# Gate tiles of four feed-forwards computed in pairs by one level of Strassen's algorithm

## The chip, the cores and the metric

The kernel runs on one core of a Trainium2 chip. The metric is the device time of one execution in microseconds (us). Three executions of the kernel before took 2094.15, 2095.79 and 2096.93 us; the median is 2095.79 us.

## What is computed

The reference is a decoder trunk of two layers over 512 tokens of 1024 channels, all in float32. Each layer is a feed-forward, a mixer (a convolution module in layer 0, sparse attention in layer 1), a second feed-forward and a gated input embedding:

```python
def rms_norm(x, g):
    y = xf * lax.rsqrt(jnp.mean(xf * xf, axis=-1, keepdims=True) + RMS_EPS)
    return y * g
def swiglu(x, wg, wu, wd):
    return (jax.nn.silu(x @ wg) * (x @ wu)) @ wd
for i in range(2):
    x = x + 0.5 * swiglu(rms_norm(x, ffn1_norm[i]), ffn1_w_gate[i], ffn1_w_up[i], ffn1_w_down[i])
    x = x + (conformer_conv if i == 0 else nsa_mixer)(rms_norm(x, mix_norm[i]), ...)
    x = x + 0.5 * swiglu(rms_norm(x, ffn2_norm[i]), ffn2_w_gate[i], ffn2_w_up[i], ffn2_w_down[i])
    gate = jax.nn.sigmoid(rms_norm(x, ple_norm[i]) @ ple_w_gate[i])
    x = x + gate * (p[i] @ ple_w_in[i])
return rms_norm(x, final_norm)
```

So there are four feed-forwards. Their weights are 1024 x 2816 (gate, up) and 2816 x 1024 (down). The change concerns `x @ wg` in all four.

## The kernel before

Activations lie transposed: eight tiles `xs[k]` of 128 channels by 512 tokens. A matrix product keeps a 128 x 128 block of weights stationary on TensorE (PE) and moves a tile of 512 tokens past it. To keep float32's precision with the faster fp32r format, each operand is split in a high part (a rounded copy) and a low part (the difference), and `mm3` issues three matmuls (L254, L255, L256): high by high, high by low, low by high.

Weights come in units of 128 x 1024 (eight blocks), numbered in the order of use. SyncE loads a unit into one of two `raw` buffers. `_split` makes the high part on ScalarE (ACT, L230) and the low part (L231) on GpSimd (POOL) for the feed-forwards, apart from the first six units, which VectorE (DVE) does. High and low parts have five buffers each (`wh`, `wl`), so a unit is split while TensorE works four units earlier.

A feed-forward has 22 gate tiles and 22 up tiles of 24 matmuls each (eight channel blocks by three). They run in two parts, f = 0 to 11 and 12 to 21; after each part come eight down tiles m, each summed over the part's f. VectorE finishes each tile f: gate times R, up times R, their product, and the hidden tile's low part, with Silu and the high part on ScalarE.

R is the RMS norm's factor per token. It isn't applied to x before the products but to their results, so the products need not wait for it. It is made by `rfin` in two steps. Step one: the squares' sum `acc`, in two parts, goes through two matmuls with a matrix of 1/1024 (L355); VectorE takes the diagonals of the result in four pieces (L347), adds epsilon (L357); POOL takes the power (L331). Step two (`spread`): four transposes on TensorE (L363) and a copy on ScalarE (L370). The constant `FIN_AT` puts step one behind the gate tile of f = 1 and step two behind the gate tile of f = 2:

```python
            at = 2 * f - (p is pg)
            if at in FIN_AT:        # FIN_AT = (1, 3)
                next(fin)
```

The order within each engine is made when the program is built, by a scheduler that starts from the order of the code; on the chip each engine then runs its instructions in that order.

The functions that the change touches, and what calls them:

Of the kernel before, what the change touches and what calls it, by code (L numbers as in the profile page):

```python
# [27 lines left out]
CALM_FROM = 6  # L28
CALM = ("ffn", "ple_w_gate", "conv_w_pw2")
# [9 lines left out]
PARTS = (range(0, 12), range(12, 22))  # L39
HU = 1024  # L40
# [15 lines left out]
def plan():  # L56
# [13 lines left out]
    def ffn(n, i):  # L70
        for fs in PARTS:
            for f in fs:
                for nm in ("gate", "up"):
                    for k in range(KD):
                        put((f"ffn{n}_w_{nm}", i, k, f), k, ((f * 128, f * 128 + 128),))
# [66 lines left out]

SMALL = {}
# [18 lines left out]
class Kern:  # L162
    def __init__(self, ctx, tc, aps):
# [12 lines left out]
        self.RAWB, self.HLB = 2, 5  # L176
# [19 lines left out]

    def _load(self, j):
        if KINDS[j] == "r":
            return ()
        return self._pieces_in(j)  # L200

    def _pieces_in(self, j):
        t = self.wpool.tile([128, HU], F32, name=f"raw{j}", tag="raw", bufs=self.RAWB)
# [6 lines left out]
    def pieces(self, j, w):  # L210
        return (slice(0, w // 2), slice(w // 2, w)) if j == 0 else (slice(0, w),)

    def _split(self, j):
        w = sum(x[2] for x in UNITS[j])
        if KINDS[j] == "r":
            t = self.wpool.tile([128, HU], F32, name=f"wr{j}", tag="wh", bufs=self.HLB)
            self.nc.sync.dma_start(t[:, :w], self.a["w"][j, :, :w])
            self.hl[j] = (t, t)
            return
        t = self.raw.pop(j)  # L220
        h = self.wpool.tile([128, HU], F32R, name=f"wh{j}", tag="wh", bufs=self.HLB)
        l = self.wpool.tile([128, HU], F32R, name=f"wl{j}", tag="wl", bufs=self.HLB)
        what = UNITS[j][0][0][0]
        nsa, calm = what.startswith("nsa"), j >= CALM_FROM and what.startswith(CALM)
        eng = self.nc.gpsimd if calm or nsa and j % 4 in L_POOL else self.nc.vector
        for c in self.pieces(j, w):
            if nsa and j % 4 in H_POOL:
                self.nc.gpsimd.tensor_copy(h[:, c], t[:, c])
            else:
                self.nc.scalar.activation(h[:, c], t[:, c], AF.Copy)  # L230
# [3 lines left out]
    def ahead(self, j):  # L234
        while self.next_split < min(j + 1, len(UNITS)):
            while self.next_raw < min(self.next_split + self.RAWB, len(UNITS)):
                drain(self._load(self.next_raw))
                self.next_raw += 1
            self._split(self.next_split)
            self.next_split += 1  # L240
        while self.next_raw < min(self.next_split + self.RAWB, len(UNITS)):
            drain(self._load(self.next_raw))
            self.next_raw += 1

    def block(self, key):
        j, o, w = PLACE[key]
        self.ahead(j + self.HLB - 1)
# [15 lines left out]
    def load_consts(self):  # L263
# [16 lines left out]
        first = [self._load(0), self._load(1)]  # L280
# [20 lines left out]
    def parts(self, k):  # L301
# [5 lines left out]
        h, l = (self.ptile("px", 16, dt=F32R) if self.gname == "ple_norm" else self.slot(F32R) for _ in range(2))  # L307
# [89 lines left out]

    def ffn(self, n, i, nxt):
        nc = self.nc
        X = self.X  # L400
        g, u, d = (f"ffn{n}_w_{s}" for s in ("gate", "up", "down"))
        fin = self.rfin(self.acc)
        for pi, fs in enumerate(PARTS):
            hid = {}

            def finish(f, pg, pu):
                R = self.R
                gr, ur = self.tmp(), self.tmp()
                nc.vector.tensor_tensor(gr, pg, R, op=OP.mult)  # L409
                nc.scalar.activation(gr, gr, AF.Silu)  # L410
                nc.vector.tensor_tensor(ur, pu, R, op=OP.mult)  # L411
                nc.vector.tensor_tensor(ur, ur, gr, op=OP.mult)  # L412
                h, l = self.ptile("hid", 24, dt=F32R), self.ptile("hid", 24, dt=F32R)
                nc.scalar.activation(h, ur, AF.Copy)  # L414
                nc.vector.tensor_tensor(l, ur, h.bitcast(F32), op=OP.subtract)  # L415
                hid[f] = (h, l)

            for f in fs:
                pg, pu = self.bank(), self.bank()
                if f == 0:  # L420
                    for ks in (range(KD - 1), (KD - 1,)):
                        for p, nm in ((pg, g), (pu, u)):
                            for k in ks:
                                self.mm3(p, self.block((nm, i, k, f)), X[k], k == 0, k == KD - 1)
                    wait = [(f, pg, pu)]
                    if 0 in FIN_AT:
                        next(fin)
                    continue
                for p, nm in ((pg, g), (pu, u)):
                    for k in range(KD):  # L430
                        self.mm3(p, self.block((nm, i, k, f)), X[k], k == 0, k == KD - 1)
                    at = 2 * f - (p is pg)
                    if at in FIN_AT:
                        next(fin)
                        if at == FIN_AT[1]:
                            for t in wait:
# [885 lines left out]
```

## Time and profile before

| | |
|---|---|
| median of three runs | 2095.79 us |
| profiled execution | 2095.87 us |
| its span, first to last instruction | 2094.1 us |
| TensorE busy | 2060.0 us, 98% |
| VectorE, ScalarE, GpSimd busy | 956.3, 830.6, 1031.2 us |

The profile names an instruction by engine, line and the program's tiles (out<-in). A matmul's duration in it runs to a modelled end and overlaps the next one's, so what a matmul costs in a stream is read from start to start. PE is TensorE's matmuls, PEld its weight loads. PEclk is the clock that the chip granted to TensorE, as a share of 2.4 GHz.

### The profile page before, as it was taken

Reading aid. Unit: us, or ns where it says so; the run is one execution under the profiler, and the core shown is the slowest. Engines: PE = TensorE matmul, PEld = TensorE weight load, DVE = VectorE, ACT = ScalarE, POOL = GpSimd, SP = SyncE. Lnnn points to the kernel's source line nnn. Section 1 sums busy time; section 2 is a strip of 40 time slices with the busy share of each in tenths; the row PEclk is TensorE's granted clock in tenths of the full one; section 3 lists DMA queues with packets and bytes.
Section 4 is the critical chain, followed back from the end, with each engine's and each line's share of the span. In section 5 each row is a group of like instructions: output and inputs, shape, how many; then the busy total and the mean of one; then the engine's idle time right before and its main releaser. Section 6 shows DMA issues by size and latency. Waiting matters only on the chain. (4 is left out here: it accounts for less than half of the span.)

```text
span 2094.1 us, 25510 instructions
## 1 busy us (share of the span) xinstructions
PE 2060.0 (98%) x9608; PEld 1709.4 (82%) x9608; DVE 956.3 (46%) x1744; ACT 830.6 (40%) x1394; POOL 1031.2 (49%) x646
## 2 busy tenths in 40 slices
PE   8999999999999999999999999999999999999998
PEld 7888888888788888887888888887888788888887
DVE  5430334597634303336432133346989653213334
ACT  5321334663533222334332223326888643223333
POOL 2444443686345444444444445647666444444442
PEclk9999999999999999999999999999999999999999
DMA  4332333244273222233332333453323033233232
GB/s 164 100 101 92 100 98 99 94 133 151 101 208 121 92 100 96 96 101 105 101 101 92 99 97 99 161 164 111 91 82 106 32 116 101 95 97 101 92 100 76
DMA packets 77322, 223.29 MB, mean 107 GB/s; under 512 B 8624, under 2 KB 16592, under 8 KB 77200
## 3 DMA queue, kind: packets, MB, share of 16 engines
q1 hardware_dynamic: 76208, 219.26, 32.8%
q0 software_dynamic: 848, 2.34, 0.3%
q8 instruction: 76, 1.25, 0.3%
q14 instruction: 46, 0.38, 0.1%
q10 hardware_dynamic: 144, 0.07, 0.0%
HBM read 203.25 MB, written 16.29 MB: 105 GB/s over the span
## 5 line engine op out<-in xcount | busy, mean ns | idle before, releaser
L231 POOL TENSOR_TENSOR wl<-raw,wh 128x1024 fp32r<-128x1024 f32 x311 | 777.5, 2501 | 858.1 <-ACT wh L230 840.4
L230 ACT ACTIVATE wh<-raw 128x1024 fp32r<-128x1024 f32 (+1 forms) x331 | 348.8, 1056 | 920.5 <-PE b L255 819.1
L254 PE MATMUL b<-s,wh 128*128 128x512 f32 x1728 | 675.3, 392 | 6.6 <-ACT s L308 5.8
L255 PE MATMUL b<-s,wh 128*128 128x512 f32 x1728 | 673.7, 390 | 1.5 <-DVE s L309 1.2
L256 PE MATMUL b<-s,wl 128*128 128x512 f32 x1728 | 673.8, 390 | 0.0
L254 PEld LDWEIGHTS b<-s,wh 128*128 128x128 f32 x1728 | 325.1, 188 | 75.4 <-ACT s L308 7.5
L255 PEld LDWEIGHTS b<-s,wh 128*128 128x128 f32 x1728 | 324.8, 188 | 69.6 <-DVE s L309 2.6
L256 PEld LDWEIGHTS b<-s,wl 128*128 128x128 f32 x1728 | 324.8, 188 | 67.7
L254 PE MATMUL b<-hid,wh 128*128 128x512 f32 x704 | 273.9, 389 | 0.0
L256 PE MATMUL b<-hid,wl 128*128 128x512 f32 x704 | 273.2, 389 | 0.0
L255 PE MATMUL b<-hid,wh 128*128 128x512 f32 x704 | 273.2, 389 | 0.0
L411 DVE TENSOR_TENSOR t<-b,R 128x512 f32<-128x512 f32 x88 | 60.7, 690 | 348.5 <-PE b L256 348.5
L415 DVE TENSOR_TENSOR hid<-t,hid 128x512 fp32r<-128x512 f32 x88 | 173.1, 1970 | 55.5 <-ACT hid L414 55.3
L451 DVE SCALAR_TENSOR_TENSOR s<-b,s 128x512 f32<-128x512 f32 x64 | 44.3, 692 | 326.5 <-PE b L256 326.5
L256 PEld LDWEIGHTS b<-hid,wl 128*128 128x128 f32 x704 | 132.1, 188 | 27.5
L255 PEld LDWEIGHTS b<-hid,wh 128*128 128x128 f32 x704 | 132.1, 188 | 27.5
L254 PEld LDWEIGHTS b<-hid,wh 128*128 128x128 f32 x704 | 132.1, 188 | 27.3
L409 DVE TENSOR_TENSOR t<-b,R 128x512 f32<-128x512 f32 x88 | 60.7, 690 | 157.6 <-PE b L256 94.6
L1033 POOL TENSOR_SCALAR e<-e,sm,gates 128x512 f32<-128x512 f32 (+3 forms) x96 | 61.5, 646 | 40.9 <-DVE sm L1027 35.2
L414 ACT ACTIVATE hid<-t 128x512 fp32r<-128x512 f32 x88 | 55.4, 631 | 54.5 <-DVE t L412 54.5
L412 DVE TENSOR_TENSOR t<-t,t 128x512 f32<-128x512 f32 x88 | 68.5, 782 | 8.0 <-ACT t L410 0.2
L308 ACT ACTIVATE s<-s,small 128x512 fp32r<-128x512 f32 x48 | 38.0, 798 | 76.7 <-DVE s L451 34.5
(223 smaller groups left out, 2245.9 us busy)
## 6 DMA issues: line engine op xcount, KB each, us to landing
raw<-in_w SPq DMA_DIRECT2D x335, 512.0 KB, 3.5
skew<-table SPq DMA_DIRECT2D x16, 320.0 KB, 9.9
z<-t SPq DMA_DIRECT2D x16, 256.0 KB, 2.2
z<-z SPq DMA_DIRECT2D x16, 256.0 KB, 3.4
tt<-skew SPq DMA_DIRECT2D x16, 256.0 KB, 2.9
wr<-in_w SPq DMA_DIRECT2D x8, 512.0 KB, 3.7
q<-t SPq DMA_DIRECT2D x32, 128.0 KB, 2.9
s<-in_xT SPq DMA_DIRECT2D x8, 256.0 KB, 6.8
```

The lines of the kernel that those rows point to most:

```text
L230: self.nc.scalar.activation(h[:, c], t[:, c], AF.Copy)
L231: eng.tensor_tensor(l[:, c], t[:, c], h[:, c].bitcast(F32), op=OP.subtract)
L254: mm(out, sh, mh, start=start, stop=False)
L255: mm(out, sh, ml, start=False, stop=False)
L256: mm(out, sl, mh, start=False, stop=stop)
L409: nc.vector.tensor_tensor(gr, pg, R, op=OP.mult)
L411: nc.vector.tensor_tensor(ur, pu, R, op=OP.mult)
L412: nc.vector.tensor_tensor(ur, ur, gr, op=OP.mult)
L414: nc.scalar.activation(h, ur, AF.Copy)
L415: nc.vector.tensor_tensor(l, ur, h.bitcast(F32), op=OP.subtract)
L451: nc.vector.scalar_tensor_tensor(self.xs[m], p, 0.5, self.xs[m], op0=OP.mult, op1=OP.add)
L1033: nc.gpsimd.tensor_scalar(dst, dst, sm[:, a, bi:bi + 1], gate, op0=OP.mult, op1=OP.mult)
```

## The change

**Pairs of gate tiles.** From f = 2 on, gate tiles are made in pairs by `gate_pair`. The pair's 256 output channels, the 1024 input channels and the 512 tokens are each halved. Seven half-size products take the place of eight, each over four channel blocks and 256 tokens, so 7 x 4 x 3 = 84 matmuls of 256 columns replace 2 x 24 of 512. The weights' sums are made from two raw units by `combine` (kinds "c" and "d"; "s" is the unit used as it is), the moving sums of x by `right_sums`, once per feed-forward, after the plain tiles f = 0 and f = 1. The results are put together by VectorE in a tile G.

**Low parts on VectorE.** POOL no longer makes the low parts of feed-forward weights; VectorE does.

**Three down parts** instead of two (f = 0 to 7, 8 to 15, 16 to 21). In each, m = 0 and 1 run together, with the part's last two f at the end. R is no longer applied to the up tile but to the down tile's result, which costs a second VectorE instruction for each. Pool sizes: 4 temporaries instead of 8, 16 hidden tiles instead of 24.

**Step two of `rfin`** now comes behind the gate tile of f = 1, before its up tile; step one behind the tiles of f = 0.

```diff
-CALM = ("ffn", "ple_w_gate", "conv_w_pw2")
+CALM = ("ple_w_gate", "conv_w_pw2")
-PARTS = (range(0, 12), range(12, 22))
+PARTS = (range(0, 8), range(8, 16), range(16, 22))
+PLAIN, HIDS = 2, 16
...
+    def combine(self, what, j):
+        t, u = self.raw[j], self.raw[j + 1]
+        lo, hi = slice(0, HU // 2), slice(HU // 2, HU)
+        if what == "c":
+            s1 = self.S1 = self.ptile("s1", 2)
+            nc.vector.tensor_tensor(s1, u[:, lo], u[:, hi], op=OP.add)
+            nc.vector.tensor_tensor(u[:, lo], t[:, lo], u[:, lo], op=OP.subtract)
+            nc.vector.tensor_tensor(t[:, lo], s1, t[:, lo], op=OP.subtract)
+            nc.vector.tensor_tensor(t[:, hi], t[:, hi], t[:, lo], op=OP.subtract)
+        src = t if what == "c" else u
+        h, l = self.halves()
+        nc.scalar.activation(h, src, AF.Copy)
+        nc.vector.tensor_tensor(l, src, h.bitcast(F32), op=OP.subtract)
+        if what == "d":
+            hl = self.ptile("s1hl", 2, HU, F32R)
+            nc.scalar.activation(hl[:, lo], self.S1, AF.Copy)
+            nc.vector.tensor_tensor(hl[:, hi], self.S1, hl[:, lo].bitcast(F32), op=OP.subtract)
...
+    def right_sums(self, name, i, k):
+        a, b, t12, t34 = (self.tmp() for _ in range(4))
+        for t, kk in ((a, k), (b, k + 4)):
+            nc.scalar.activation(t, self.xs[kk], AF.Copy, scale=self.col(name, i * KD + kk))
+        sub(t12[:, lo], a[:, hi], a[:, lo])
+        sub(t12[:, hi], b[:, hi], t12[:, lo])
+        sub(t34[:, lo], b[:, hi], a[:, hi])
+        sub(t34[:, hi], b[:, lo], t12[:, hi])
+        for t in (t12, t34):
+            p = self.ptile("px", 8, HU, F32R)
+            nc.scalar.activation(p[:, :512], t, AF.Copy)
+            sub(p[:, 512:], t, p[:, :512].bitcast(F32))
...
+    def gate_pair(self, g, i, f):
+        product(C[:, lo], "s", 0, B11)
+        nc.scalar.activation(u, C[:, lo], AF.Copy)
+        product(A[:, lo], "s", 1, B21)
+        product(A[:, hi], "c", 0, T2)
+        add(G4[:, :, 0], two(A), twice(u))
+        product(C[:, hi], "e", 0, T1)
+        add(v, C[:, hi], G4[:, 1, 0])
+        product(B[:, lo], "c", 1, B22)
+        product(B[:, hi], "d", 0, T3)
+        add(G4[:, 1, 0], B[:, hi], G4[:, 1, 0])
+        add(G4[:, :, 1], two(B), twice(v))
+        product(C[:, lo], "d", 1, T4)
+        add(G4[:, 1, 0], C[:, lo], G4[:, 1, 0])
...
+                for f in range(PLAIN):
+                    pg, pu = self.bank(), self.bank()
+                    for ks in (range(KD - 1), (KD - 1,)) if f == 0 else (range(KD),):
+                        plain(pg, g, f, ks)
+                        if f == 1:
+                            next(fin)
+                        plain(pu, u, f, ks)
+                    wait.append((f, pg, pu))
+                    if f == 0:
+                        next(fin)
+                    for k in (2 * f, 2 * f + 1):
+                        self.right_sums(f"ffn{n}_norm", i, k)
...
-                nc.vector.scalar_tensor_tensor(self.xs[m], p, 0.5, self.xs[m], op0=OP.mult, op1=OP.add)
+                    nc.vector.scalar_tensor_tensor(p[m], p[m], 0.5, R, op0=OP.mult, op1=OP.mult)
+                    nc.vector.tensor_tensor(self.xs[m], p[m], self.xs[m], op=OP.add)
```

How this moves instructions is shown at the start of layer 1's first feed-forward. TensorE before: L355 are the two matmuls of step one, L363 the transposes of step two; the 65 rows left out are matmuls of the plain tiles.

```order
L355 MATMUL b_7100<-t_7002,meanr 128x512
L255 MATMUL b_7068<-s_6746,wh_6913 128x512
L256 MATMUL b_7068<-s_6745,wl_6914 128x512
L254 MATMUL b_7068<-s_6758,wh_6913 128x512
L355 MATMUL b_7100<-t_7003,meanr 128x512
L255 MATMUL b_7068<-s_6759,wh_6913 128x512
...
L255 MATMUL b_7142<-s_6992,wh_7008 128x512
L256 MATMUL b_7142<-s_6991,wl_7009 128x512
L363 MATMUL b_7174<-ident,r 128x128 x4
L254 MATMUL b_7143<-s_6745,wh_7035 128x512
```

Between the second L355 and L363 stand 68 matmuls here. TensorE now, at the same place (L434 is what L355 was, L442 what L363 was; L329 to L331 are the three matmuls of `mm3`):

```order
L331 MATMUL b_8309<-s_8140,wl_8106 128x512
L434 MATMUL b_8265<-t_8193,meanr 128x512
L329 MATMUL b_8309<-s_8181,wh_8105 128x512
L330 MATMUL b_8309<-s_8182,wh_8105 128x512
L331 MATMUL b_8309<-s_8181,wl_8106 128x512
L442 MATMUL b_8342<-ident,r 128x128 x4
L329 MATMUL b_8310<-s_7937,wh_8148 128x512
```

Three matmuls stand between them now, and the up tile of f = 1 (b_8310) follows the transposes. In the other three feed-forwards, in the order of execution layer 0 first, layer 0 second, layer 1 second, there were 50, 72 and 61 matmuls between, and are now 3, 28 and 3.

VectorE before, at the same place: the four pieces of the diagonal (L347) and the epsilon (L357), behind the low part of the squares' sum (L379).

```order
L379 TENSOR_TENSOR t_7003<-acc_6749,t_7002 128x512
L347 ISA junk,v<-b_7100,ident 128x128
L347 ISA v 128x1
L347 ISA junk,v<-b_7100,ident 128x128
L347 ISA v 128x1
L347 ISA junk,v<-b_7100,ident 128x128
L347 ISA v 128x1
L347 ISA junk,v<-b_7100,ident 128x128
L347 ISA v 128x1
L357 TENSOR_SCALAR v<-v 128x4
```

They stood one behind the other. VectorE now, from the third piece on (L426 is what L347 was, L436 what L357 was; L484 is `right_sums`, L299 the low part of combined weights, L281 that of plain ones):

```order
L426 ISA junk,v<-b_8265,ident 128x128
L426 ISA v 128x1
L484 TENSOR_TENSOR t_8295<-t_8294,t_8295 128x256
L484 TENSOR_TENSOR t_8296<-t_8294,t_8293 128x256
L299 TENSOR_TENSOR wl_8233<-raw_8109,wh_8232 128x1024
L426 ISA junk,v<-b_8265,ident 128x128
L426 ISA v 128x1
L484 TENSOR_TENSOR t_8296<-t_8294,t_8295 128x256
L299 TENSOR_TENSOR wl_8312<-rawx_8198,wh_8311 128x1024
L281 TENSOR_TENSOR wl_8350<-raw_8200,wh_8349 128x1024
L436 TENSOR_SCALAR v<-v 128x4
```

From the first piece to L436 there are now twelve other instructions between: six of 128 x 256, three of 128 x 512 and three of 128 x 1024. In layer 1's second feed-forward they are the same, in layer 0's first three, one and three, in layer 0's second six, five and three.

## Rows read from the trace of the kernel before

**Rows 1.** The page: span, then busy us, share and instructions by engine.

```profile
span 2094.1 us, 25510 instructions
PE 2060.0 (98%) x9608; PEld 1709.4 (82%) x9608; DVE 956.3 (46%) x1744; ACT 830.6 (40%) x1394; POOL 1031.2 (49%) x646
```

**Rows 2.** Busy time by stretch, most of layer 1's first feed-forward.

```profile
core 0: us, PE busy (x) PEld busy (x) DVE busy (x) ACT busy (x) POOL busy (x), PEclk, DMA share, GB/s
1015.00:1300.00 285.00, 285.00 (x1260) 235.96 (x1260) 94.66 (x96) 83.33 (x99) 132.17 (x52) 1.00 0.30 97
```

**Rows 3.** Timeline of PE, the same feed-forward: start us, us, engine, line, tiles.

```profile
1210.03 0.39 PE L254 MATMUL b<-s,wh 128*128 128x512 f32 x1
...
1215.47 0.39 PE L254 MATMUL b<-s,wh 128*128 128x512 f32 x1
```

**Rows 4.** Timeline of PE in the final stage, matmuls of 256 columns.

```profile
2061.75 0.28 PE L254 MATMUL b<-px,wh 128*128 128x256 f32 x1
2061.87 0.28 PE L255 MATMUL b<-px,wh 128*128 128x256 f32 x1
...
2065.70 0.28 PE L254 MATMUL b<-px,wh 128*128 128x256 f32 x1
```

**Rows 5.** Busy time by stretch there; matmuls of 128 columns by line.

```profile
2065.00:2070.00 5.00, 5.00 (x44) 5.00 (x43) 3.42 (x8) 2.82 (x7) 0.00 (x0) 1.00 0.20 54
...
L636 PE MATMUL b<-uu,tw 128*128 128x128 f32 x360 | 41.1, 275 | 1.1 <-DMA uu<-ud 1.1
```

**Rows 6.** Timeline of DVE: instructions of 512, 1024 and 256 columns.

```profile
17.09 0.68 DVE L325 TENSOR_TENSOR acc<-acc,t 128x512 f32<-128x512 f32 x1
17.69 1.22 DVE L231 TENSOR_TENSOR wl<-raw,wh 128x1024 fp32r<-128x1024 f32 x1
18.82 0.68 DVE L325 TENSOR_TENSOR acc<-acc,t 128x512 f32<-128x512 f32 x1
...
2068.05 0.42 DVE L1225 TENSOR_TENSOR t<-t,z 128x256 f32<-128x256 f32 x1
2068.50 0.43 DVE L1226 TENSOR_TENSOR s<-s,t 128x256 f32<-128x256 f32 x1
2068.84 0.42 DVE L1225 TENSOR_TENSOR t<-t,z 128x256 f32<-128x256 f32 x1
```

**Rows 7.** Timeline of DVE at the start of layer 1's first feed-forward.

```profile
996.88 0.75 DVE L309 SCALAR_TENSOR_TENSOR s<-s,small,s 128x512 fp32r<-128x512 f32 x1 [0.79 <-ACT s L308]
...
1000.62 0.29 DVE L347 CUSTOM_DVE_ANT_0 junk<-b,ident 128x128 f32<-128x128 f32 x1 [1.01 <-PE b L355]
...
1001.96 0.39 DVE L357 TENSOR_SCALAR v<-v 128x4 f32<-128x4 f32 x1
```

**Rows 8.** Timeline there of PE (steps one and two of R) and POOL.

```profile
1000.08 0.40 PE L355 MATMUL b<-t,meanr 128*128 128x512 f32 x1
1015.74 0.60 PE L363 MATMUL b<-ident,r 128*128 128x128 f32 x4
...
1004.63 1.00 POOL L331 TENSOR_TENSOR r<-v,power 128x4 f32<-128x4 f32 x1
```

**Rows 9.** Timeline of PE at the kernel's start.

```profile
9.91 0.79 PE L254 MATMUL b<-s,wh 128*128 128x512 f32 x1 [3.87 <-ACT s L308]
...
11.29 0.63 PE L256 MATMUL b<-s,wl 128*128 128x512 f32 x1
11.71 0.64 PE L254 MATMUL b<-s,wh 128*128 128x512 f32 x1
...
15.22 0.40 PE L254 MATMUL b<-s,wh 128*128 128x512 f32 x1
```

**Rows 10.** Busy time by stretch at the start and in the convolution stage.

```profile
10.00:15.00 5.00, 4.84 (x10) 2.99 (x11) 4.90 (x7) 5.00 (x9) 0.00 (x0) 0.50 0.64 247
532.00:540.00 8.00, 7.59 (x33) 5.79 (x32) 4.87 (x8) 8.00 (x14) 0.03 (x1) 1.00 0.18 68
```

**Rows 11.** Timeline of PE in the convolution stage.

```profile
528.72 0.65 PE L363 MATMUL b<-ident,r 128*128 128x128 f32 x4 [2.92 <-POOL r L331]
```

**Rows 12.** The page: the costliest groups by line; DMA issues.

```profile
L231 POOL TENSOR_TENSOR wl<-raw,wh 128x1024 fp32r<-128x1024 f32 x311 | 777.5, 2501 | 858.1 <-ACT wh L230 840.4
L230 ACT ACTIVATE wh<-raw 128x1024 fp32r<-128x1024 f32 (+1 forms) x331 | 348.8, 1056 | 920.5 <-PE b L255 819.1
...
raw<-in_w SPq DMA_DIRECT2D x335, 512.0 KB, 3.5
```

More of the change, by code (lines that the diff above doesn't have):

```diff
@@ L71, in ffn @@
         for fs in PARTS:
+            order = [(nm, f) for f in fs if f < PLAIN for nm in ("gate", "up")]
             for f in fs:
-                for nm in ("gate", "up"):
-                    for k in range(KD):
-                        put((f"ffn{n}_w_{nm}", i, k, f), k, ((f * 128, f * 128 + 128),))
+                if f >= PLAIN and f % 2 == 0:
+                    order += [("gate", f), ("gate", f + 1), ("up", f), ("up", f + 1)]
+            for nm, f in order:
+                for k in range(KD):
+                    put((f"ffn{n}_w_{nm}", i, k, f), k, ((f * 128, f * 128 + 128),), "s" if nm == "up" or f < PLAIN else "ab"[f % 2])
             for m in range(KD):
@@ L141, with splits @@
 UNITS, KINDS, PLACE = plan()
+def splits():
+    order, entry = [], {}
+    for j, kind in enumerate(KINDS):
+        if kind == "a":
+            entry[j], entry[j + 1] = len(order), len(order) + 2
+            order += [("s", j), ("c", j), ("d", j)]
+        elif j not in entry:
+            entry[j] = len(order)
+            order.append((kind, j))
+    last = {}
+    for e, (what, j) in enumerate(order):
+        last[j + (what == "d")] = e
+    return order, entry, last
+SPLITS, ENTRY, LAST = splits()
+RAWS = {tag: [j for j, kind in enumerate(KINDS) if kind in kinds] for tag, kinds in (("raw", "sa"), ("rawx", "b"))}
+BEFORE = {j: js[n - 2] if n > 1 else None for js in RAWS.values() for n, j in enumerate(js)}
 SMALL = {}
@@ L208, in _pieces_in, with loads @@
             yield
-    def pieces(self, j, w):
-        return (slice(0, w // 2), slice(w // 2, w)) if j == 0 else (slice(0, w),)
-    def _split(self, j):
+    def loads(self):
+        while self.next_raw < len(UNITS):
+            j = self.next_raw
+            if KINDS[j] == "r":
+                if ENTRY[j] > self.next_split:
+                    return
+            elif BEFORE[j] is not None and LAST[BEFORE[j]] >= self.next_split or KINDS[j] == "b" and not self.here(j):
+                return
+            drain(self._load(j))
+            self.next_raw += 1
@@ L214, in _split, with here, halves @@
+    def here(self, j):
+        return UNITS[j][0][0][:2] == self.now
+    def halves(self):
+        h = self.wpool.tile([128, HU], F32R, name=f"wh{self.uid}", tag="wh", bufs=self.HLB)
+        l = self.wpool.tile([128, HU], F32R, name=f"wl{self.uid}", tag="wl", bufs=self.HLB)
+        self.uid += 1
+        return h, l
+    def _split(self, what, j):
+        nc = self.nc
         w = sum(x[2] for x in UNITS[j])
-        if KINDS[j] == "r":
+        if what == "r":
             t = self.wpool.tile([128, HU], F32, name=f"wr{j}", tag="wh", bufs=self.HLB)
-            self.nc.sync.dma_start(t[:, :w], self.a["w"][j, :, :w])
+            nc.sync.dma_start(t[:, :w], self.a["w"][j, :, :w])
@@ L218, in _split @@
             self.hl[j] = (t, t)
             return
[L220 to L225, printed above, removed]
+        if what in "cd":
+            self.combine(what, j)
+            return
@@ L240, in ahead @@
+    def ahead(self, e):
+        free = min(self.held | {e}) + self.HLB
+        e = min(e + self.HLB, free, len(SPLITS))
+        self.loads()
+        while self.next_split < e:
+            what, j = SPLITS[self.next_split]
+            if what in "cd" and not self.here(j):
+                return
+            self._split(what, j)
             self.next_split += 1
-        while self.next_raw < min(self.next_split + self.RAWB, len(UNITS)):
-            drain(self._load(self.next_raw))
-            self.next_raw += 1
+            self.loads()
@@ L306, in parts @@
         g = self.col(self.gname, self.gi * KD + k)
-        h, l = (self.ptile("px", 16, dt=F32R) if self.gname == "ple_norm" else self.slot(F32R) for _ in range(2))
+        if self.gname == "ple_norm":
+            t = self.ptile("px", 8, HU, F32R)
+            h, l = t[:, :512], t[:, 512:]
+        else:
+            h, l = self.slot(F32R), self.slot(F32R)
         nc.scalar.activation(view(h), x, AF.Copy, scale=g)
```

157 lines of the change are left out of this document (95 added, 62 removed).

## The prediction

> **What bounds the kernel now.** I read the page's busy line first. TensorE works 2060.0 us of a span of 2094.1 [rows 1]; the reader is to see that no other engine is above half, so what counts is TensorE's stream of matmuls and its holes. Next the busy time by stretch: in 285 us of a feed-forward TensorE has no idle time at all, while VectorE is busy for 94.66 and GpSimd for 132.17 [rows 2]. The feed-forwards are bound by TensorE alone. Then the timeline, for what a matmul costs: 24 steps of 512 columns take 5.44 us, 0.2267 us each [rows 3]. In the final stage 33 steps of 256 columns take 3.95 us, 0.1197 each [rows 4], more than half of 0.2267: there the weight loads are busy all the time, and matmuls of 128 columns, 41.1 us for 360, cost 0.114 [rows 5]. Narrower matmuls hardly come cheaper.
>
> **The pairs.** A pair of gate tiles costs 48 x 0.2267 = 10.88 us now and 84 x 0.1197 = 10.05 after: 0.83 us less, where seven products for eight would suggest 1.36. Each feed-forward has 10 pairs (f = 2 to 21), so 40 pairs give back 33.1 us. The price of a pair's matmul is bounded by 0.114 below (1.30 us a pair, 52 us in all) and, if loads cost more here, by the point of no gain, 0.1295; I take 0.1197, as these are the same instructions on the same shapes. The Trainium skill (TensorE: Matmul & The Clock Gate, Back-to-back issue gap) gives an isolated gap of N/2.4 + 2.5 ns. By it a pair would go from 10.4 to 9.2 us, an estimate from that page, and the 40 pairs would give 48 us; the trace has both steps longer, so the rows decide.
>
> **What VectorE takes over, in a steady pair.** By [rows 6], start to start, 1024 columns cost 1.13 us, 512 columns 0.60, 256 columns 0.34 to 0.45, say 0.40. A pair has six instructions of 1024 (five low parts, gate times R), eleven of 512 (four sums and one low part of weights, two additions for G, two products, two hidden low parts) and three of 256: 6.8 + 6.6 + 1.2 = 14.6 us, or 16 with the full durations. TensorE needs 10.05 + 10.88 = 20.9 us for the pair and its two up tiles, so VectorE has 5 us left. One wait stands in its queue: a sum of a new unit waits for a load of 3.5 us [rows 12] that starts only when the buffer's former low part is done. It fits into the 5 us, and the next products' weights are made a pair ahead. ScalarE's share is some 9 us a pair (1.06 for 1024 columns [rows 12]). So steady pairs cost TensorE nothing; without that cover each microsecond of lateness would cost 40. GpSimd's 2.5 us low parts [rows 12] leave the feed-forwards, and nothing waited for them there: gain nothing. The second instruction for each down tile (0.60) and the third part hide in the same way: a down tile of six f lasts 18 x 0.2267 = 4.1 us, against 3.5 us of VectorE's work even where the next norm is prepared, and at a part's start 24 to 36 matmuls (5.4 to 8.2 us) run before the last two hidden tiles are wanted, some 2.5 us of work. The bytes loaded are the same.
>
> **Step two of R, the added wait.** Before, layer 1's first feed-forward ran its second mean matmul at 1000.08, the diagonal began at 1000.62, and the epsilon came at 1001.96 [rows 7, 8]; the power ran on GpSimd from 1004.63 for 1.00 us; the transposes came at 1015.74, ten microseconds after R's root was there. Now the order has three matmuls, 0.7 us, between mean and transposes. And the diagonal's four pieces, 1.34 us together, no longer follow each other: six instructions of 256, three of 512 and three of 1024 stand between, 2.4 + 1.8 + 3.4 = 7.6 us. From the mean's start the root needs 0.54 + 1.34 + 7.6 + 0.39 (epsilon) + 1.00 (power) = 10.9 us; TensorE gets there in 0.23 + 0.68 = 0.9. **It waits 9.9 us**, and behind the transposes stand the up tile of f = 1 and everything else on TensorE; ScalarE's copy of R and with it VectorE's finishing of f = 0 and 1 wait too. By the order's counts the same sum gives:
> - layer 1, second feed-forward: the same rows, 9.9 us;
> - layer 0, first: three of 256, one of 512, three of 1024, 5.2 us in place of 7.6: 7.6 us of waiting;
> - layer 0, second: six, five and three, 8.8 us; VectorE comes 3.2 us late to the first piece (four of 512, two of 256), but 28 matmuls (6.3 us) stand between: 3.2 + 1.34 + 8.8 + 1.4 - 6.6 = 8.1 us.
>
> Together 35.5 us. Below, the wait is bounded by the chain with nothing in between (0.54 + 1.34 + 0.39 + 1.00 - 0.9 = 2.4 us a start, 9.5 in all); above by the instructions' full durations (0.69 and 1.22 in place of 0.60 and 1.13, so about 1 us more a start) and by waits for ScalarE: 45.
>
> **What is late next.** If the root came in time, the sums of x would not. From the low part of the last x tile to that of the last sum T2, VectorE has 21 instructions of 512, 16 of 256, three of 1024 and the diagonal: 12.6 + 6.4 + 3.4 + 1.5 = 23.9 us. TensorE gets to that sum after 54 matmuls of 512 columns, the means, the transposes and 33 matmuls of 256: 12.2 + 0.5 + 0.6 + 4.0 = 17.3. So 6.6 us would be waited there. After the longer wait for R it is covered: from the epsilon on TensorE needs 11 us to T2, VectorE 9.2.
>
> **The clock.** At the kernel's start TensorE was idle for 3.87 us [rows 9]; then the granted clock was 0.50, the 1.2 GHz level [rows 10], and steps of 512 columns took 0.42 us, until 15.22, 5.3 us after it resumed [rows 9]. In the convolution stage it was idle for 2.92 us [rows 11], and the clock afterwards was 1.00 [rows 10]. Idle times of 8 to 10 us are like the first, so each of the four starts should lose 5.3 x (1 - 0.2267/0.42) = 2.4 us more, 9.6 in all; between nothing, as after the short idle time, and that. The Trainium skill (TensorE: Matmul & The Clock Gate, Why this matters for your kernels) warns against idle gaps between bursts of matmuls for this reason; both of these idle times agree with it.
>
> **The sum**, on the profiled execution of 2095.87 us (1.8 us around its span, and 0.1 us from the median, so nothing is to be converted): 2095.9 - 33.1 + 35.5 + 9.6 = 2107.9, so **2108 us**, 0.6% slower.
>
> **The rivals.**
> - *Faster: the starts cost little.* If TensorE waited at each start only as long as it did at 528.72, 2.92 us, and kept its clock, the sum is 2095.9 - 33.1 + 11.7 = 2074.5. For it speaks that the diagonal alone took 1.34 us before; against it that the order puts 7.6 us of work between its pieces and that an engine runs its queue in order. It wins if the starts cost under 8.3 us each, clock included; the sums of x alone would take 6.6.
> - *No change: the waits are as summed, but the clock stays.* 2095.9 + 2.4 = 2098.3; with the waits at 6.6 us and the clock's loss, 2095.9 - 33.1 + 26.4 + 9.6 = 2098.8. Rows 11 speak for it, the longer idle time of rows 9 against.
> - *Slower still: the pairs give nothing.* Weight loads fill the whole time at 256 columns [rows 5]. If a step cost 0.1295, or if VectorE came 0.83 us late in each pair, the gain is gone: 2095.9 + 45 = 2141. Half of it gives 2124. Rows 4 speak against the first, the 5 us left in each pair against the second; a stall of over 1.1 us a pair would be slower even without the starts.
> - *That it doesn't do what it says* can be left out: the order has 1920 fewer matmuls of 512 columns and 3360 more of 256, as counted above.
>
> **How the numbers follow.** The forecast has 0.62, with its own range of 2100 to 2119; slower still 0.09; no change 0.12; faster 0.17. A measurement can't tell changes below 0.2% or 4.2 us, so same means 2091.6 to 2100.0. Hence faster 0.18, same 0.13, slower 0.69. For the range I leave out most of the slower-still case and the lower half of the faster one: 2077 to 2123.
>
> **What would show it.** Idle time of TensorE before L442, ended by GpSimd's power L410, of 8 to 10 us at four places; the clock at 0.5 for some 5 us behind each; steps of 0.12 us in the 256-column matmuls and no idle time inside the steady pairs; the diagonal's pieces (L426) spread over some 9 us. TensorE's busy time should fall by about 33 us less the clock's loss, while the span grows. The prediction is wrong if the idle time before L442 is under 5 us, or if steady pairs show holes, or if a pair's products take more than 10.5 us.

## The result

The changed kernel takes 2111.87 us (median of four executions, 2110.39 to 2118.73), the kernel before 2096.36 on the same chip: a ratio of 1.0080, 95% interval 1.0056 to 1.0105, so 15.5 us slower. The profiled execution took 2111.71 us with a span of 2109.9.

The page, to be read against [rows 1]:

```profile
span 2109.9 us, 29020 instructions
PE 2041.1 (97%) x11048; PEld 1762.0 (84%) x11048; DVE 1431.8 (68%) x2538; ACT 937.9 (44%) x1538; POOL 382.0 (18%) x388
```

TensorE's busy time fell by 18.9 us while the span grew by 15.8: it waits longer. The list of waits of PE names for whom (waited for: us in total, times, longest us):

```profile
PE b L442 <- POOL r L410: 38.7, 6, 9.1
```

L442 is the transposes of step two of R, L410 GpSimd's power. Four of the six are the starts of the feed-forwards. The timeline of PE at the start of layer 1's first one answers to [rows 8]:

```profile
1007.15 0.40 PE L434 MATMUL b<-t,meanr 128*128 128x512 f32 x1
1007.38 0.39 PE L329 MATMUL b<-s,wh 128*128 128x512 f32 x1
1007.61 0.40 PE L330 MATMUL b<-s,wh 128*128 128x512 f32 x1
1007.85 0.40 PE L331 MATMUL b<-s,wl 128*128 128x512 f32 x1
1017.34 1.12 PE L442 MATMUL b<-ident,r 128*128 128x128 f32 x4 [9.09 <-POOL r L410]
1018.11 0.78 PE L329 MATMUL b<-s,wh 128*128 128x512 f32 x1
...
1022.52 0.53 PE L330 MATMUL b<-s,wh 128*128 128x512 f32 x1
1022.89 0.40 PE L331 MATMUL b<-s,wl 128*128 128x512 f32 x1
```

Mean matmul, three followers, nine empty microseconds, then 11 matmuls that take 4.78 us instead of 2.49. From the first piece of the diagonal to the epsilon VectorE is never idle. Its timeline and GpSimd's, against [rows 7, 8]:

```profile
1007.58 0.29 DVE L426 CUSTOM_DVE_ANT_0 junk<-b,ident 128x128 f32<-128x128 f32 x1 [0.20 <-PE b L434]
...
1009.08 0.69 DVE L304 TENSOR_TENSOR s1hl<-s,s1hl 128x512 fp32r<-128x512 f32 x1
1009.68 0.28 DVE L426 CUSTOM_DVE_ANT_0 junk<-b,ident 128x128 f32<-128x128 f32 x1
...
1010.83 0.28 DVE L426 CUSTOM_DVE_ANT_0 junk<-b,ident 128x128 f32<-128x128 f32 x1
...
1011.71 1.22 DVE L299 TENSOR_TENSOR wl<-raw,wh 128x1024 fp32r<-128x1024 f32 x1
1012.84 0.28 DVE L426 CUSTOM_DVE_ANT_0 junk<-b,ident 128x128 f32<-128x128 f32 x1
...
1013.39 1.22 DVE L299 TENSOR_TENSOR wl<-rawx,wh 128x1024 fp32r<-128x1024 f32 x1
1014.52 1.22 DVE L281 TENSOR_TENSOR wl<-raw,wh 128x1024 fp32r<-128x1024 f32 x1
1015.66 0.16 DVE L436 TENSOR_SCALAR v<-v 128x4 f32<-128x4 f32 x1
...
1015.90 1.38 POOL L410 TENSOR_TENSOR r<-v,power 128x4 f32<-128x4 f32 x1 [48.76 <-DVE v L436]
```

The four pieces of the diagonal (L426) are spread from 1007.58 to 1013 among the weight sums and low parts; the epsilon comes 8.1 us after the first piece, where it came after 1.34 before. The other three starts look alike; by start-to-start gaps the four waits are 6.8, 9.2, 9.3 and 9.3 us, 34.5 together (what a step lasts anyway taken off). The clock comes back sooner at the other three: after 6, 9 and 7 matmuls of the up tile. The first start, where the wait is 6.8 us:

```profile
36.65 1.12 PE L442 MATMUL b<-ident,r 128*128 128x128 f32 x4 [6.64 <-POOL r L410]
37.41 0.78 PE L329 MATMUL b<-s,wh 128*128 128x512 f32 x1
...
39.97 0.39 PE L329 MATMUL b<-s,wh 128*128 128x512 f32 x1
```

Busy time by stretch (columns as in [rows 2]): the clock behind the wait, and a steady part of eight tiles between two rounds of down tiles.

```profile
1019.30:1020.30 1.00, 1.00 (x4) 0.80 (x3) 0.77 (x2) 0.00 (x0) 0.00 (x0) 0.50 0.43 172
1023.30:1024.30 1.00, 1.00 (x6) 0.78 (x6) 1.00 (x4) 0.35 (x1) 0.00 (x0) 1.00 0.00 0
1132.38:1216.37 83.99, 83.99 (x530) 76.33 (x528) 58.08 (x76) 33.06 (x39) 0.00 (x0) 1.00 0.36 111
```

In the last row TensorE has no idle time at all. Its 83.99 us hold eight up tiles (8 x 24 x 0.2267 = 43.5) and four pairs: 10.12 us a pair, 0.1205 a step.

One place was not foreseen. Behind layer 1's first feed-forward, timelines of DVE, PE and POOL:

```profile
1346.87 3.02 DVE L388 SCALAR_TENSOR_TENSOR s<-s,small,s 128x512 fp32r<-128x512 f32 x1 [0.79 <-ACT s L387]
...
1354.49 2.27 DVE L1018 CAST wh<-wl 128x384 fp32r<-128x384 f32 x1
...
1361.65 0.50 PE L329 MATMUL b<-s,wh 128*128 128x512 f32 x1 [1.21 <-ACT s L387]
1362.65 0.50 PE L330 MATMUL b<-s,wh 128*128 128x512 f32 x1 [0.50 <-DVE s L388]
...
1346.93 2.41 POOL L281 TENSOR_TENSOR wl<-raw,wh 128x1024 fp32r<-128x1024 f32 x1
...
1354.15 2.39 POOL L281 TENSOR_TENSOR wl<-raw,wh 128x1024 fp32r<-128x1024 f32 x1 [1.47 <-ACT wh L280]
```

Two VectorE instructions took 3.02 and 2.27 us (the same L388 takes 0.75 elsewhere), each beside a low part that GpSimd still makes for the attention's weights. The last x tile was late, TensorE lost 2.1 us, and then ran at half clock (PEclk 0.50 from 1365 to 1367).

### The profile page after: what moved, and what is told of

Read it like the earlier page. It is cut to its first block, busy times and chain, and to the rows that moved or that the text cites. A ratio compares the mean times of both kernels' runs of the same rounds, so it can differ in the third digit from the quotient of the medians.

```text
span 2109.9 us, 29020 instructions
## 1 busy us (share of the span) xinstructions
PE 2041.1 (97%) x11048; PEld 1762.0 (84%) x11048; DVE 1431.8 (68%) x2538; ACT 937.9 (44%) x1538; POOL 382.0 (18%) x388
## 4 chain that ended last, share of the span: by engine, by line
PE 63%; DVE 6%; ACT 3%; issue 2%; DMA 1%; POOL 0%; SPq 0%; POOLq 0%; DVEq 0%; ACTq 0%
PE b L329 20%; PE b L330 20%; PE b L331 20%; PE b L1144 1%; DVE t L1209 1%; PE b L1206 1%; PE b L1083 1%; ACT e L1164 1%; DVE s L388 1%; PE b L1225 0%; ACT t L1208 0%; PE b L1226 0%; DVE wl L281 0%; ACT ec L1164 0%; DVE e L1162 0%
## 5 line engine op out<-in xcount | busy, mean ns | idle before, releaser
L329 PE MATMUL b<-s,wh 128*128 128x512 f32 (+1 forms) x1568 | 566.6, 362 | 4.5 <-ACT s L387 3.4
L330 PE MATMUL b<-s,wh 128*128 128x512 f32 (+1 forms) x1568 | 565.3, 361 | 1.7 <-DVE s L388 1.4
L331 PE MATMUL b<-s,wl 128*128 128x512 f32 (+1 forms) x1568 | 563.9, 360 | 0.0
L281 DVE TENSOR_TENSOR wl<-raw,wh 128x1024 fp32r<-128x1024 f32 (+1 forms) x245 | 306.9, 1254 | 70.7 <-ACT wh L280 64.8
L329 PEld LDWEIGHTS b<-s,wh 128*128 128x128 f32 x1568 | 299.5, 191 | 49.2 <-ACT s L387 5.1
L330 PEld LDWEIGHTS b<-s,wh 128*128 128x128 f32 x1568 | 299.5, 191 | 44.1 <-DVE s L388 2.6
L331 PEld LDWEIGHTS b<-s,wl 128*128 128x128 f32 x1568 | 299.0, 191 | 42.6
L331 PE MATMUL b<-hid,wl 128*128 128x512 f32 x704 | 274.0, 389 | 0.0
L329 PE MATMUL b<-hid,wh 128*128 128x512 f32 x704 | 273.3, 389 | 0.0
L281 POOL TENSOR_TENSOR wl<-raw,wh 128x1024 fp32r<-128x1024 f32 (+1 forms) x53 | 126.6, 2392 | 721.7 <-ACT wh L280 711.7
L329 PE MATMUL b<-px,wh 128*128 128x256 f32 (+1 forms) x632 | 190.1, 301 | 0.0
L331 PE MATMUL b<-px,wl 128*128 128x256 f32 (+1 forms) x632 | 189.9, 301 | 0.0
L330 PE MATMUL b<-px,wh 128*128 128x256 f32 (+1 forms) x632 | 189.8, 301 | 0.0
L603 DVE SCALAR_TENSOR_TENSOR b<-b,R 128x512 f32<-128x512 f32 x96 | 66.5, 697 | 174.4 <-PE b L331 174.4
L331 PEld LDWEIGHTS b<-hid,wl 128*128 128x128 f32 x704 | 132.2, 188 | 27.4
L329 PEld LDWEIGHTS b<-hid,wh 128*128 128x128 f32 x704 | 132.2, 188 | 27.4
L551 DVE TENSOR_TENSOR b<-b,G 128x512 f32<-128x512 f32 x80 | 55.7, 698 | 113.7 <-PE b L331 113.7
L329 PEld LDWEIGHTS b<-px,wh 128*128 128x128 f32 x632 | 120.7, 191 | 5.6
L330 PEld LDWEIGHTS b<-px,wh 128*128 128x128 f32 x632 | 120.7, 191 | 5.7
```

The costliest lines, as they stand in the source:

```text
L281: eng.tensor_tensor(l[:, c], t[:, c], h[:, c].bitcast(F32), op=OP.subtract)
L329: mm(out, sh, mh, start=start, stop=False)
L330: mm(out, sh, ml, start=False, stop=False)
L331: mm(out, sl, mh, start=False, stop=stop)
L551: nc.vector.tensor_tensor(pu, pu, gr, op=OP.mult)
L603: nc.vector.scalar_tensor_tensor(p[m], p[m], 0.5, R, op0=OP.mult, op1=OP.mult)
```

## The experiments

Ratios are to the kernel before on the same chip, with 95% intervals. Microseconds gained or lost against the changed kernel are taken from the ratios.

**1. Step two later.** At f = 1, R's transposes are asked for behind the up tile:

```diff
-                        if f == 1:
-                            next(fin)
                         plain(pu, u, f, ks)
...
+                next(fin)
                 R = self.R
```

> The changed kernel with step two of R behind the up tile of f = 1, so 24 matmuls (5.44 us) more stand between the second mean matmul and the transposes at each of the four starts; VectorE's queue is almost unchanged. My theory: the waits before the transposes, 6.8, 9.2, 9.3 and 9.3 us in the changed kernel, are the latency of R's chain through VectorE, so they shrink by 5.4 each to about 1.4, 3.7, 3.8 and 3.8 (21.8 us back in all), but then the first product with T2 follows the transposes after only 33 matmuls of 256 columns, some 6.2 us behind the epsilon against 9.2 us of VectorE's work, and TensorE waits about 3 us there at each start (12 us given back again). About 2097 us in all, 2090 to 2102 with the clock open. Rival (the wait for R is the only cost of the starts): no wait at T2, about 2080. Second rival (the waits don't depend on where the transposes stand): no change, 2112.

2081.91 us, 0.9939 (0.9924 to 0.9954), 29.6 us back, close to the rival's 2080. The waits are 1.4, 1.7, 3.8 and 3.8 us, as my theory had them, but for the second (3.7); behind the first two the granted clock is 1.00, behind the third and fourth 0.50. First and third:

```profile
36.58 0.65 PE L442 MATMUL b<-ident,r 128*128 128x128 f32 x4 [1.21 <-POOL r L410]
...
1004.11 0.65 PE L442 MATMUL b<-ident,r 128*128 128x128 f32 x4 [3.66 <-POOL r L410]
```

T2 is the first sum of x that a pair's products read. In front of a product with a sum of x only one start has a hole, 2.5 us. So the wait follows the place of the transposes, and the sums of x are mostly not late. Some 4 of the 29.6 us don't belong to the starts: against the changed kernel's trace they lie behind layer 1's first feed-forward and in the attention stage.

**2. The diagonal kept together.** VectorE's work traced between the two steps is put behind the epsilon:

```diff
...
+                        with self.tc.issue_after(self.eps) if f == 1 else nullcontext():
                             plain(pg, g, f, ks)
...
+                    with self.tc.issue_after(self.eps):
                         for k in (2 * f, 2 * f + 1):
```

> The changed kernel with VectorE's sums of x and combinations of the weights traced after step one of R held behind the epsilon, so that between the diagonal's four pieces stands one instruction of 1024 columns instead of 5.2 to 8.8 us of work; TensorE's order stays the same. My theory: the waits before the transposes fall from 6.8, 9.2, 9.3 and 9.3 us to about 2.7, 1.5, 3.7 and 3.7 (23 us back), and the work that was held back, some 6.5 us, is then in front of T2, where TensorE waits 4 to 7 us at each start: the sum moves little, about 2104 us (2095 to 2112). Rival (the interleaving is the whole cost, the sums of x are covered): about 2079 with the clock regained.

2095.19 us, 0.9998 (0.9989 to 1.0007), 17 us back, between the two theories. The list of waits:

```profile
PE b L443 <- POOL r L411: 13.6, 6, 3.1
PE b L330 <- ACT t L579: 4.2, 2, 2.1
...
PE b L330 <- ACT px L493: 1.8, 1, 1.8
```

25 of 38.7 us of waiting for the root are gone, although between the mean and the transposes TensorE has almost as few matmuls as in the changed kernel (6, 28, 3 and 3 for 3, 28, 3 and 3). So the interleaving explains these 25 us; some 10 are left at the starts, for the rest of the chain. Holding work back opens three new holes of about 2 us (the second and third row), only one of them at a sum of x (px), against the 4 to 7 us at each start that I expected.

**3. A shorter chain for R.**

```diff
-        fin = self.rfin(self.acc)
+        fin = self.rfin(self.acc, True)
```

> The changed kernel with R's mean taken by four one-column matmuls per token block straight from the float32 sum (as the second norm of the layers already does elsewhere in the kernel) instead of two 512-column matmuls and the diagonal: the sum is ready earlier, VectorE has one instruction of 4 columns in the chain, and 24 to 36 matmuls stand between it and the transposes. My theory: no wait before the transposes at all and no fall of the clock there (34.5 and about 10 us back), but then the sums of x are late: TensorE waits 4 to 7 us before the product with T2 at each start, about 22 us: 2089 us (2080 to 2094). Rival (nothing else is late): 2067. Second rival (the root is late again, since VectorE has a queue in front of its one instruction): over 2100.

2071.60 us, 0.9884 (0.9867 to 0.9900), 41 us back. No wait before the four transposes, and one hole of 2.15 us in place of four. It isn't at T2 either: it stands in front of the next product, with T1 (weights s1hl), and was ended by a copy on ScalarE (run 9 has more on it):

```profile
608.43 0.48 PE L329 MATMUL b<-px,s1hl 128*128 128x256 f32 x1 [1.99 <-ACT t L522]
```

Why T2 isn't late, in the timelines of PE and DVE at layer 1's first feed-forward (px is a sum of x, s with 512 columns an up tile):

```profile
1010.73 0.28 PE L331 MATMUL b<-px,wl 128*128 128x256 f32 x1
1011.33 0.50 PE L329 MATMUL b<-s,wh 128*128 128x512 f32 x1 [0.32 <-ACT t L576]
...
1017.27 0.27 PE L330 MATMUL b<-px,wh 128*128 128x256 f32 x1
...
1012.51 1.29 DVE L484 TENSOR_TENSOR px<-t,px 128x512 fp32r<-128x512 f32 x2
```

In the changed kernel's order the 12 matmuls with T2 follow one another; in this program's, 48 matmuls of up tiles stand among them. VectorE wrote the last sum's low parts at 1012.5 to 1013.8, 29 us after the last x tile's, later than the forecast 24; but TensorE read that of T2 at 1017.27, 34 us after, not 17.

**4. Parts of 6, 8 and 8 tiles.**

```diff
-PARTS = (range(0, 8), range(8, 16), range(16, 22))
+PARTS = (range(0, 6), range(6, 14), range(14, 22))
```

> The changed kernel with the feed-forward's three parts of 6, 8 and 8 tiles instead of 8, 8 and 6, so that a down tile of the last part, beside which the next norm is prepared, lasts 24 matmuls (5.44 us) instead of 18 (4.1 us). My theory: behind layer 1's first feed-forward VectorE came late with the last x tile (a wait of 2.1 us on TensorE at 1361 and about 1.8 us at half clock behind it); with 5.44 us per tile its 3.6 us chain keeps up, and 4 us come back: 2108 us. Rival (that wait comes from elsewhere, such as GpSimd's low parts of the next stage's weights): no change, 2112. If the other feed-forwards' ends had hidden losses too, below 2105.

2105.78 us, 1.0048 (1.0033 to 1.0063), 6 to 7 us back. The wait at 1361 and the half clock behind it are gone, 4 us by the traces; the four waits for R are as they were. Where the other 2 to 3 us come from isn't shown.

**5. Three and four together.** The two edits above.

> The mean by one-column matmuls and the parts of 6, 8 and 8 tiles together. My theory: the two losses are separate (the starts, and the last x tile before layer 1's attention), so the gains add: 2071.6 us less the 6 that the parts gave alone, 2065.6 us, 1.4% under the kernel before. Rival (both touch the same slack on VectorE): 2070 or more.

2069.36 us, 0.9871 (0.9856 to 0.9886): the fastest kernel measured, 27 us under the one before. From run 3 to here the gain is some 3 us, not 6, and the intervals overlap: whether the two add is not settled. The wait behind layer 1's first feed-forward went; the hole at 608, in front of T1's product, grew from 2.15 to 3.25 us.

**6. Idle time filled.** 30 matmuls on a constant, which nobody reads, in front of the transposes:

```diff
...
+            if fill:
+                p = self.bank()
+                with self.tc.issue_after(self.mm):
+                    for n in range(fill):
+                        self.nc.tensor.matmul(p, self.meanr, ...)
             self.R = self.spread(r)
...
-        fin = self.rfin(self.acc)
+        fin = self.rfin(self.acc, fill=30)
```

> The changed kernel with 30 matmuls of 512 columns on a constant, whose result nobody reads, put between the second mean matmul's three followers and the transposes at each of the four starts (6.8 us at 0.2267 us each). They don't bring R any earlier: TensorE is idle for about 0, 2.4, 2.4 and 2.4 us in front of the transposes instead of 6.8 to 9.3, and the transposes run when they ran before. My theory: the clock then stays at its upper level behind three or all four starts, and the 2.6 us that each lost at half clock come back: 2101.5 us (2101 to 2106 if some of the short idle times still cost the clock). Rival (the half clock behind the waits belongs to something else, such as the transposes themselves): no change, 2112, or more where the filler is in the way.

2106.07 us, 1.0047 (1.0030 to 1.0063), 7 us back. Behind three of the four starts the granted clock is now 1.00, and by the traces 6.5 of the 8.2 us that it cost at the starts are gone. At three starts R comes no earlier than in the changed kernel, at the second some 2.5 us earlier; so the whole 7 us are not the clock, but these 6.5 are. Against that earlier R stands a new hole of 2.4 us in the same feed-forward, in front of a pair's last product (at 624.36, behind a raw load that VectorE waited 4.1 us for). At the remaining start the clock fell after all, at about 1017.4, behind a short idle time:

```profile
1016.04 0.65 PE L442 MATMUL b<-ident,r 128*128 128x128 f32 x4 [2.28 <-POOL r L410]
...
1017.50 0.63 PE L330 MATMUL b<-s,wh 128*128 128x512 f32 x1
1017.93 0.63 PE L331 MATMUL b<-s,wl 128*128 128x512 f32 x1
```

**7. GpSimd keeps the low parts of plain units**, from the seventh unit on, on top of run 5:

```diff
-CALM = ("ple_w_gate", "conv_w_pw2")
+CALM = ("ffn", "ple_w_gate", "conv_w_pw2")
...
-        nsa, calm = name.startswith("nsa"), name.startswith(CALM)
+        nsa, calm = name.startswith("nsa"), j >= 6 and name.startswith(CALM)
```

> The kernel of the run before last's expectation (one-column mean, parts of 6, 8 and 8) with the low parts of the feed-forwards' plain units, up and down weights, on GpSimd as in the kernel before; the low parts of the combined units stay on VectorE. My theory: in the feed-forwards VectorE had time to spare and GpSimd too, so the engine makes no difference: within 4 us of 2065.6. Rival one (VectorE was the hidden bound of the pairs): 10 us or more faster. Rival two (GpSimd's 2.4 us low parts slow VectorE's instructions beside them, as one of 3.02 us instead of 0.75 at 1346.87 suggests): slower by more than 4 us.

2102.51 us, 1.0029 (1.0016 to 1.0042), 33 us slower than run 5: rival two, and far more than I gave it. Steady parts are as long as before (83.92 us); the loss is at the starts and ends. One reason is in the timeline of POOL, beside a VectorE that is busy without a pause from 1003 to 1014:

```profile
1007.59 7.75 POOL L410 TENSOR_TENSOR r<-v,power 128x4 f32<-128x4 f32 x1 [10.20 <-DVE v L466]
```

**8. The short chain in the kernel before.** The edit of run 3.

> The kernel before the change, with only the feed-forwards' mean taken by one-column matmuls as in the third run. My theory: there R had ten microseconds to spare, so the shorter chain gives back only the idle times of about 2.9 us at the starts of layer 1 (990 to 998, and 1682): 2092 to 2096 us; the difference to the pairs with the same mean, 22 us or more, is then what the pairs give. Rival (the short chain is a gain of its own, and the pairs give little): 2080 or less.

2097.39 us, 1.0008 (0.9999 to 1.0018): no change. The short chain is worth nothing by itself. Against this kernel run 3, the change with the same short chain, is 26 us faster, and run 5, with run 4's parts besides, 29.

**9. Table loads moved**, on top of run 5: `skew_next` only in the second and third part, each load behind the last raw load (`issue_after`).

> The one-column mean and the parts of 6, 8 and 8, and the 16 table loads of 320 KB that the second feed-forward of layer 0 issues for the attention spread, two behind a raw load at each pair of its second and third part, instead of all within some 25 us at its start. There the trace of the fifth run shows the DMA engines busy for 20 us without a break, a raw load of 512 KB landing after 7.7 us instead of 3.6, ScalarE's queue waiting 4.35 us for it and TensorE 3.25 us at 608.37, with half clock behind that. My theory: that hole and its half clock go, 4 us: 2065 us (2063 to 2067). Rival (the loads only collide with others later): no change, 2069. Second rival: steady pairs that wait for raw loads now show holes, over 2071.

2070.80 us, 0.9878 (0.9863 to 0.9893): no change, for a reason that no theory had. The hole at 608 is gone, but with loads on time VectorE no longer pauses, and there is a new wait (POOL and PE):

```profile
587.59 9.24 POOL L410 TENSOR_TENSOR r<-v,power 128x4 f32<-128x4 f32 x1 [17.38 <-DVE v L466]
...
596.88 0.48 PE L442 MATMUL b<-ident,r 128*128 128x128 f32 x1 [4.01 <-POOL r L410]
```

The same power takes 1.00 us in [rows 8].

**10. Only the low parts moved to VectorE, in the kernel before.**

```diff
-CALM = ("ffn", "ple_w_gate", "conv_w_pw2")
+CALM = ("ple_w_gate", "conv_w_pw2")
```

> The kernel before the change with one part of the change alone: the low parts of the feed-forwards' weights on VectorE instead of GpSimd. My theory: both engines have time to spare there and R's root has ten microseconds, so nothing changes: 2094 to 2099 us. Rival one (VectorE's fuller queue delays the root or the last x tile): 2101 or more. Rival two (GpSimd's low parts slowed VectorE's instructions beside them at the starts and ends): 2092 or less.

2088.81 us, 0.9965 (0.9952 to 0.9978), 7 to 8 us faster: rival two. In the kernel before, timelines of DVE and POOL:

```profile
982.74 2.88 DVE L498 TENSOR_TENSOR t<-t,z 128x512 f32<-128x512 f32 x1
...
982.23 2.84 POOL L231 TENSOR_TENSOR wl<-raw,wh 128x1024 fp32r<-128x1024 f32 x1 [0.56 <-ACT wh L230]
```

and without GpSimd's low part beside it:

```profile
976.45 0.68 DVE L498 TENSOR_TENSOR t<-t,z 128x512 f32<-128x512 f32 x1
```

There the last x tile comes in time, and the idle times at 990 to 998, 2.9 us together, are gone; 3 us more come back in the attention stage and at the start of the feed-forward behind it, for which no row is shown.

**11. Only three parts, in the kernel before**: `PARTS` as in the change.

> The kernel before the change with three parts of 8, 8 and 6 tiles instead of 12 and 10, its down tiles in one VectorE instruction as before. A down tile of the last part lasts 4.1 us; VectorE's chain beside it takes about 2.9 us. My theory: it keeps up, apart from the one instruction that took 3.0 us at 1349.80 beside GpSimd's low parts, so at most 2 us are lost: 2095 to 2099 us. Rival (a third part costs 4 us by itself): 2100 or more.

2104.61 us, 1.0035 (1.0023 to 1.0046), 7 to 8 us slower: the rival. Timelines of DVE and PE behind layer 1's first feed-forward:

```profile
1345.12 5.38 DVE L309 SCALAR_TENSOR_TENSOR s<-s,small,s 128x512 fp32r<-128x512 f32 x1 [0.79 <-ACT s L308]
...
1355.26 0.50 PE L254 MATMUL b<-s,wh 128*128 128x512 f32 x1 [1.23 <-ACT s L308]
1358.28 0.79 PE L255 MATMUL b<-s,wh 128*128 128x512 f32 x1 [2.52 <-DVE s L309]
```

Shorter down tiles leave no slack for instructions of 5.38 and 2.99 us, and half clock follows (0.50 from 1359 to 1363).

**12. VectorE pauses for the power**, on top of run 9: a copy of R's root in VectorE's queue, later work behind it.

```diff
...
+                        self.held_at = self.nc.vector.tensor_copy(r, q).ins
...
```

> The kernel of the ninth run with one copy of four columns on VectorE that reads R's root and stands in VectorE's queue one to three instructions behind the sum's epsilon, with everything traced later behind it: VectorE pauses until GpSimd's power is done. In the ninth run that power took 9.24 us in the second feed-forward of layer 0, beside 17 VectorE instructions without a pause between them, and TensorE waited 4.18 us for it at 596.88; where VectorE had little to do it took 1.03. My theory: GpSimd's four columns don't get through beside VectorE's two-input instructions; with the pause every power takes 1.0 to 2 us, that wait and the half clock behind it go, and VectorE's pause of 1 to 2 us a start is covered: 2065 us (2063 to 2067). Rival one (the power's length has to do with the loads or the trace and not with VectorE): the power stays at 9 us, VectorE stands still as long, and the sums of x are late: over 2075. Rival two (the pause makes the sums of x late): the power is short, and TensorE waits at T1 or T2: 2068 to 2073.

2076.43 us, 0.9907 (0.9890 to 0.9923), slower than runs 5 and 9. On the power the forecast holds:

```profile
586.68 1.47 POOL L411 TENSOR_TENSOR r<-v,power 128x4 f32<-128x4 f32 x1 [13.82 <-DVE v L467]
```

1.47 us for 9.24, and no wait for R at the starts. On the time it doesn't: the held queue makes the sums late (2.2 us at 49.65, some 5 us in four pieces from 1011 to 1017), rival two with a worse price than it named.

## Why the prediction was right, and where it was not

The forecast was 2108 us, with slower as the likeliest outcome; it came to 2111.87. Step by step:

| term | forecast | measured | by |
|---|---|---|---|
| 40 pairs | -33.1 | -30.4 | 0.1205 us a step, 10.12 a pair |
| four waits for R | +35.5 | +34.5 | gaps at L442; runs 1 to 3 |
| half clock behind them | +9.6 | +8.2 | 1.5 + 2.1 + 2.7 + 1.9 us, run 6 |
| sum | +12.0 | +12.3 | whole change: +15.5; its trace: +15.8 |
| low parts off GpSimd | 0 | -7.8 by themselves | run 10, in the kernel before |
| third part | 0 | +8.0 by itself | run 11, in the kernel before |

Each of the forecast's three terms came to within 3 us, and their sum to 0.3. What the trace of this one execution has beyond them, 3.5 us, lies elsewhere: 4.0 behind layer 1's first feed-forward, 1.9 in the convolution stage and 0.6 in attention, less the 2.9 us of idle time at 990 to 998 that the changed kernel no longer has. The last two rows are not part of the sum: they were measured in the other kernel, and this trace shows only some of each (below).

**The pairs.** The step costs 0.1205 us, not 0.1197: right mechanism, 0.07 us a pair too much. Steady pairs have no holes, as said. "Slower still" is refuted by 83.99 busy of 83.99 us.

**Step two of R.** Single waits were forecast at 7.6, 8.1, 9.9 and 9.9 us and are 6.8, 9.2, 9.3 and 9.3. The cause was stated rightly: moving the transposes back (run 1) or taking the work from between the pieces (run 2) removes most of it, doing without the pieces (run 3) all. The "faster" rival named the condition, starts under 8.3 us, and run 3 meets it.

**The clock.** The start shown first loses 4.78 - 2.49 = 2.3 us in 11 matmuls, and 0.36 in the transposes (0.77 us to the next matmul against 0.41 at full clock in run 6). It is the longest of the four, though run 6's expectation took it for each: the others lose 1.5, 2.1 and 1.9 us, so the 5.3 us at half clock of [rows 9] were too long a measure for them. Filling the idle time kept the clock up at three starts.

**What is late next: this step failed.** I had TensorE waiting 6.6 us at T2 at each start once the root was early (17.3 us of its work against VectorE's 23.9). Run 3 shows no wait at T2 at all, and its one hole, of 2.15 us, has another cause. VectorE took longer than I said there, 29 us, but TensorE's side failed altogether, 34 us: the program's order is written anew when the mean changes, with two up tiles among the products with T2. A count from one program's order doesn't hold for another's.

**Two zeros that were not.** "Nothing waited for them there: gain nothing" looked for someone waiting for GpSimd's low parts; the cost was in the VectorE instruction beside them (2.88 us for 0.68). "The third part hides" set VectorE's 3.5 us against 4.1 with ordinary durations, and left out that the trace had one such instruction at 3.00 us, at 1349.80, beside a GpSimd low part. Each is worth some 8 us in the kernel before (by the intervals 5 to 10). In the changed kernel's trace less is left of them: of run 11's loss 4.0 us behind layer 1's first feed-forward, where run 11 lost 7.6 (why not as much isn't shown); of run 10's gain the 2.9 us at 990 to 998, and nothing in the attention stage. That +4.0 and -2.9 nearly cancel was luck: the forecast had both at nothing.

## What to carry to other kernels

When an edit fills an engine that was half idle, look first at the short chains that run through its queue: the pairs paid 30 us, and a four-column result stuck behind VectorE's new work took 43, clock included. Take such a result by a path that doesn't use the full engine (run 3), then ask again what is late. And an instruction that now and then lasts three or four times as long as its like is a row to explain, not an outlier: here it pointed at some 8 us each way in the kernel before.

## What the runs showed of the hardware

GpSimd and VectorE hold each other up. The power of 4 columns took 1.00 us in [rows 8], 1.38 in the changed kernel, and 7.75 and 9.24 where VectorE ran two-input instructions without a pause; both of these ended 0.9 us after VectorE's queue had stopped (at 1014.46 in run 7, at 595.92 in run 9). With a pause made for it, it took 1.47. An unbroken queue doesn't always shut it out: the 1.38 us in the changed kernel passed beside three two-input instructions with no pause between them or behind them. What sets the two cases apart stays open. The other way round, a VectorE instruction of 512 columns took 2.88 us beside a GpSimd low part of 2.84. The Trainium skill (SBUF — State Buffer, Who interferes with whom) says that VectorE and GpSimd share a second pair of ports, that a VectorE instruction with two SBUF inputs contends with a GpSimd instruction that reads SBUF, and that the pair is held as an exclusive lock. The traces agree that the two delay each other, and show more: GpSimd was kept waiting over 14 VectorE instructions in a row in run 9 (my expectation of run 12 said 17).

The length of one idle time doesn't settle what the clock does. Behind 2.92 us in the convolution stage it stayed at the upper level, 2.4 GHz, in the kernel before [rows 11], and behind 2.5 us in run 1 too; behind the same 2.92 us in the changed kernel it fell to the lower, 1.2 GHz (a mean of 0.66 from 530 to 535), and in run 6 it fell some 1.4 us after TensorE had resumed from 2.28 us. Timeline of PE and busy time by stretch in the changed kernel:

```profile
530.47 0.65 PE L442 MATMUL b<-ident,r 128*128 128x128 f32 x4 [2.92 <-POOL r L410]
...
530.00:535.00 5.00, 4.53 (x15) 3.70 (x16) 3.84 (x7) 2.29 (x4) 0.42 (x1) 0.66 0.33 108
```
